# First stage of a decoder trunk: modulation sums by transpose and ScalarE row sums, and two weight buffers moved to multiples of 512 bytes

## The chip, the cores and the metric

The program runs on one NeuronCore of a Trainium2 chip. The metric is the device time of one execution in microseconds (us). Before the change it is 685.16 us, the median of 3 runs (684.44 to 686.75). A core has five engines that each work through their own list of instructions in order and wait for one another by semaphores: TensorE (PE; its weight loads are shown apart as PEld), VectorE (DVE), ScalarE (ACT), GpSimd (POOL) and SyncE (SP, which here only issues transfers). TensorE multiplies a stationary tile, loaded as weights, by a moving tile, and writes into PSUM; all else lies in SBUF, 128 partitions wide.

## The reference

One layer of a decoder on a sequence of 512 tokens with 1024 channels. The part that the change touches is its beginning: a modulation computed from the condition `c`, a normalisation, and the first columns of the input projection.

```python
cs = jax.nn.silu(c)
mod = cs @ w_ada[l] + b_ada[l]
shift1, scale1, gate1, shift2, scale2, gate2 = [m[:, None, :] for m in jnp.split(mod, 6, axis=-1)]
h = _rmsnorm(x, norm1_g[l]) * (1.0 + scale1) + shift1
proj = h @ w_in[l]
...
merged = (jax.nn.sigmoid(ga) * (out_a @ w_branch_swa[l])
          + jax.nn.sigmoid(gd) * (out_d @ w_branch_diff[l]))
x = x + gate1 * (merged @ w_out[l])
```

After the projection come a sliding-window attention and a differential attention, each projected back (`w_branch_swa`, `w_branch_diff`), gated, merged and projected out; then a gated MLP with a short convolution, and a last normalisation. All inputs are float32.

## The kernel before

Channels are cut into eight blocks of 128, numbered k = 0 to 7. The first stage (from about 15 us to 55 us) runs over these blocks and accumulates six PSUM banks `acc6`, each 128 projected columns by 512 tokens. A float32 product is made of three products of fp32r parts: `wh*hTh`, `wl*hTh` and `wh*hTl`, where `wh`/`hTh` are rounded copies and `wl`/`hTl` what the rounding left out. `mm_k(k, 0)` issues the first two products for the banks it is given, `mm_k(k, 2)` the third; so a block costs 18 matmuls of 128x512.

What a block needs before its matmuls:

- The modulation of its 128 channels (`mod`): column 0 a scale, column 1 a shift. Each is a sum over 1024 input channels of `w_ada` times `cs`. The loaded weights `adaw[k]` hold eight slices kk for each of the two sums (j = 0 scale, j = 1 shift). Two partial sums are kept: `ac_1` starts from slice 1 and collects the odd slices, `ac_0` starts from slice 0 and collects the even ones. ScalarE (for k from 3 on) makes the two first products in `ac_first`; VectorE then adds six slices by SCALAR_TENSOR_TENSOR instructions in `ac_ops` (line L301), and adds the two partial sums (L302). What remains is a sum over the 128 partitions: TensorE multiplies `ac_0` as the stationary operand by one column of ones into `pa` (L328). VectorE then adds `1 + bias` to the scale and multiplies by the norm's gain (L334), and ScalarE adds the bias to the shift (L338).
- The turned tokens: `h_turn` transposes four 128x128 tiles of the normalised `x` into PSUM (`xt`, L379).
- `h_tile`: ScalarE applies scale and shift to `xt`, once rounded (`hTA` or `hThB`, called hT below, L384) and once in float32 (`hf`, L384). VectorE subtracts them (`h_low`, L392) and gets `hTl`.
- The weights: ScalarE rounds them (`w0h`, L362 and L364), VectorE subtracts (`w0l`, L370 and L372).

In this stage the lists of TensorE, VectorE and ScalarE stand in the order in which the code is written (`manual_schedule`). In iteration gi of the loop they get the work of block gi and the preparation of block gi+1: TensorE twelve matmuls of block gi, then `pa(gi+1)`, the four transposes of block gi+1, and the six matmuls with `hTl(gi)`; VectorE the six L301, L302, `h_low(gi)`, L334, and the splits of `w0(gi+1)`; ScalarE the two `ac_first` of block gi+2, L338, hT and hf of block gi+1, and the rounding of `w0(gi+2)`. After the stage a scheduler orders the instructions; the first weights of the next projection are rounded by ScalarE (L128, a cast of 128x1024) and subtracted by VectorE (L129). Those two are told to stand behind the instruction `last_mod`, the last one that `finish_mod` returns:

```python
with tc.issue_after(last_mod.ins):
    prefetch()
```

The buffers of the weights of odd blocks (`w0h`, `w0l` for k = 1, 3, 5, 7) lie in the pool `p1`, from byte 198272 of each partition on, which is 128 bytes past a multiple of 512; those of even blocks lie at multiples of 512. Much later (247 us to 303 us) the products with `w_branch_diff` take their weights from `wbd`, at byte 195232, 160 bytes past a multiple of 512. All other stationary operands of 128x512 matmuls lie at multiples of 512. Between the stages named here nothing of the code differs.

Of the kernel before, what the change touches and what calls it, by code (L numbers as in the profile page):

```python
# [8 lines left out]
F32 = mybir.dt.float32  # L9
F32R = mybir.dt.float32r  # L10
AF = mybir.ActivationFunctionType
ALU = mybir.AluOpType
PSUM = bass.MemoryType.PSUM

P = 128
D = 1024
S = 512
KT = D // P
# [42 lines left out]
def kernel(  # L61
# [22 lines left out]
    nc = tc.nc  # L84
# [21 lines left out]
    def tbank(name, shape=(P, S)):  # L106
        return bank("t", 2, list(shape), name)
# [34 lines left out]
    ones = cpool.tile([P, P], F32, name="ones")  # L142
    nc.gpsimd.memset(ones, 1.0)
    ident = cpool.tile([P, P], F32, name="ident")
# [31 lines left out]
    DONE = (0, 4, 2, 5, 1, 3)  # L176
# [42 lines left out]
    pp = pool("p1", stack=p1)  # L219
# [3 lines left out]
    ALONE = 3  # L223
# [50 lines left out]
    cols = cpool.tile([P, NR], F32, name="cols")  # L274
    nc.vector.tensor_copy(cols, pc)
    bsh, bsc1, n1g, sublnc = cols[:, 0:8], cols[:, 8:16], cols[:, 16:24], cols[:, 24:25]
    nc.vector.tensor_scalar_add(bsc1, bsc1, 1.0)
    nc.vector.tensor_scalar_mul(n1g, n1g, -0.5)
    nc.vector.tensor_scalar_mul(sublnc, sublnc, -0.5 * (1.0 - LAM_INIT))
    ac, mods, wts = {}, {}, {}  # L280


    def ac_first(gi, b):
        a = pp.tile([P, 2, P], F32, tag=f"ac{b}", bufs=2, name=f"ac{gi}_{b}")
        aw = adaw[gi]
        if gi < ALONE and b:
            nc.vector.tensor_scalar_mul(a, aw[:, :, b], cs[:, b : b + 1])
        else:
            nc.scalar.activation(a, aw[:, :, b], AF.Copy, scale=cs[:, b : b + 1])
        ac.setdefault(gi, {})[b] = a  # L290

    def ac_ops(gi, low):
        aw = adaw[gi]
        if gi < ALONE:
            ac_first(gi, 1)
        order = (3, 2, 5, 4) if gi == 1 else (3, 5, 2, 7, 4, 6) if gi < ALONE else (3, 2, 5, 4, 7, 6)
        for n, kk in enumerate(order):
            if gi == 1 and n == 1:
                split_lo(0, 1)
            a = ac[gi][kk % 2]  # L300
            nc.vector.scalar_tensor_tensor(a, aw[:, :, kk], cs[:, kk : kk + 1], a, ALU.mult, ALU.add)  # L301
        nc.vector.tensor_add(ac[gi][0], ac[gi][0], ac[gi][1])  # L302
        low()
# [16 lines left out]
    def reduce_mod(gi, early=None):  # L320
        pa = early or tbank(f"pa{gi}", (P, 2, P))
        for j in range(2):
            if early:
                if j:
                    direct(pa, 1, gi, (6, 7))
                nc.tensor.matmul(pa[:, j], ac[gi][0][:, j], ones, start=False, stop=True)
            else:
                nc.tensor.matmul(pa[:, j, 0:1], ac[gi][0][:, j], ones[:, 0:1], start=True, stop=True)  # L328
        return pa

    def finish_mod(k, pa):
        pa = pa if k == 0 else [pa[:, 0], pa[:, 1]]
        m = pp.tile([P, 16], F32, tag="mod", bufs=3, name=f"mod{k}")
        last = nc.vector.scalar_tensor_tensor(  # L334
            m[:, 0:1], pa[0][:, 0:1], bsc1[:, k : k + 1], n1g[:, k : k + 1], ALU.add, ALU.mult
        )
        if k:
            nc.scalar.activation(m[:, 1:2], pa[1][:, 0:1], AF.Identity, bias=bsh[:, k : k + 1])  # L338
        else:
            nc.vector.tensor_add(m[:, 1:2], pa[1][:, 0:1], bsh[:, k : k + 1])  # L340
        mods[k] = m
        return last

    def w0_views(k):
        wh, wl = wts[k]
# [35 lines left out]
    def h_tile(k, between=None):  # L381
        hf = pp.tile([P, S], F32, tag="hf", bufs=2, name=f"hf{k}")
        for dst in (hTh[k], hf):
            nc.scalar.activation(dst, pts[k], AF.Identity, bias=mods[k][:, 1:2], scale=mods[k][:, 0:1])  # L384
            if dst is not hf and between is not None:
                between()
            if dst is not hf and k + 1 < ALONE:
                ac_first(k + 1, 0)
        hfs[k] = hf

    def h_low(k):
        nc.vector.tensor_sub(hTl[k], hfs[k], hTh[k].bitcast(F32))  # L392

    FIRST = (0, 2, 1, 3, 4, 5)

    def mm_k(k, part, some=DONE):
        wh, wl = wts[k]
        last = k == KT - 1
        if part == (2 if last else 1):
            return  # L400
        for i in some:
            for p in (1, 2) if last and part else (0, 1) if part == 0 and not last else (part,):
                lhs, rhs = ((wh, hTh), (wl, hTh), (wh, hTl))[p]
                nc.tensor.matmul(
                    acc6[i], lhs[:, i * P : (i + 1) * P], rhs[k], start=k == 0 and p == 0, stop=last and p == 2
                )
# [28 lines left out]
    def scale_x(t):  # L435
        nc.scalar.activation(xn[:, t, HEAD:], xn[:, t, HEAD:], AF.Copy, scale=rst[:, t : t + 1])
# [46 lines left out]
    for gi in range(KT):  # L483
        more = gi + 1 < KT
        if more:
            if gi == 0:
                scale_x(2)
            split_hi(gi + 1)
            if gi == 1:
                scale_x(3)  # L490
            ac_ops(gi + 1, lambda: h_low(gi))
        else:
            h_low(gi)
            lp = cpool.tile([P, 2, 64], F32, name="lp")
            ls = cpool.tile([P, 2], F32, name="ls")
            nlam = cpool.tile([P, 1], F32, name="nlam")
            nc.vector.tensor_mul(lp, lamv[:, 0:4:2], lamv[:, 1:4:2])
            nc.vector.reduce_sum(ls, lp, axis=mybir.AxisListType.X)
            nc.scalar.activation(ls, ls, AF.Exp)
            nsink = cpool.tile([P, 8], F32, name="nsink")  # L500
            nc.vector.tensor_scalar_mul(nsink, sink, -1.0)
            nc.vector.tensor_sub(nlam, ls[:, 1:2], ls[:, 0:1])
            nc.vector.tensor_scalar_add(nlam, nlam, -LAM_INIT)
        if gi == 0:
            h_turn(1)
        mm_k(gi, 0, DONE if gi else FIRST[:5])
        mm_k(gi, 1)
        if more:
            if gi == 0:
                split_lo(1, 0)  # L510
            pa = reduce_mod(gi + 1, early_mod(1) if gi == 0 else None)
            if gi == 0:
                mm_k(0, 0, FIRST[5:])
            if ALONE <= gi + 2 < KT:
                ac_first(gi + 2, 1)
                ac_first(gi + 2, 0)
            if gi:
                h_turn(gi + 1)
            last_mod = finish_mod(gi + 1, pa)
            if gi:  # L520
                split_lo(gi + 1, 0)
            split_lo(gi + 1, 1)
            h_tile(gi + 1)
        mm_k(gi, 2)
# [503 lines left out]
    for i in range(SWA_PAIRS):  # L1028
        more = i + 1 < SWA_PAIRS
# [66 lines left out]
    bp = pool("mlp")  # L1096
# [32 lines left out]
        units.append((load, branch))  # L1129

    m2 = bp.tile([40, P], F32, name="m2")
    c2 = bp.tile([P, 40], F32, name="c2")
    s2c, a2c = c2[:, 0:8], c2[:, 8:16]
    nc.sync.dma_start(m2[16:32, :], b_ada[0, 3 * D : 5 * D].rearrange("(a p) -> a p", p=P))
    nc.sync.dma_start(m2[32:40, :], norm2_g[0].rearrange("(a p) -> a p", p=P))
# [396 lines left out]
    last = range(KT - TAIL, KT)  # L1532
# [213 lines left out]
    for i, (J, name) in enumerate(slots):  # L1746
# [23 lines left out]
        if i in rows_at:  # L1770
            hf = rows_at[i]
# [329 lines left out]
```

## Time and profile before

| What | Value |
| --- | --- |
| Time, median of 3 runs (lowest to highest) | 685.16 us (684.44 to 686.75) |
| Time of the profiled execution, and its span | 685.38 us, 683.6 us |
| TensorE clock granted over the span | 0.997 |
| Busy share of PE, DVE, ACT, POOL | 99%, 82%, 58%, 14% |
| Transfers | 123.87 MB, mean 181 GB/s |
| Block 3 of the first stage (31.38 to 36.40 us) | 5.02 us |
| Block 4 of the first stage (36.40 to 41.34 us) | 4.94 us |

The span runs from the first to the last instruction; the time of an execution has 1.8 us more around it. A busy PE is not yet a PE at its peak: matmuls overlap, so how closely they follow one another is read from the starts of two neighbours, not from their durations. In a timeline each row gives the start, the duration, the engine, the line, the operation, the tiles written and read, the shape, how many neighbours of the same kind were put into one row, and in brackets the idle time of the engine before it with what ended it.

### The profile page before, as it was taken

How to read it: one execution, taken by the hardware profiler on the slowest of the kernel's cores; microseconds unless marked ns; L12 is line 12 of the kernel's file. 1: busy time of each engine (PE TensorE's matmuls, PEld its weight loads, DVE VectorE, ACT ScalarE, POOL GpSimd, SP SyncE). 2: the span in 40 equal slices, each digit the busy share in tenths (PEclk: the TensorE clock that was granted, in tenths of full speed). 3: DMA queues.
4: the chain of work that ended last, by engine and by line, in shares of the span. 5: the costliest groups of instructions: out<-in, count | busy, mean ns of one | idle time of the engine just before them, and what ended most of it. 6: DMA issues, size and time to landing. Idle time of an engine off the chain costs nothing. (4 is left out here: it accounts for less than half of the span.)

```text
span 683.6 us, 10903 instructions
## 1 busy us (share of the span) xinstructions
PE 673.7 (99%) x4005; PEld 582.2 (85%) x4005; DVE 562.5 (82%) x1075; ACT 398.1 (58%) x722; POOL 98.4 (14%) x119
## 2 busy tenths in 40 slices
PE   8999999999999999999999999999999999999995
PEld 5887887878888888888899999999999998888885
DVE  4999875988796756794589988988888999979997
ACT  6776774546543223233377756666666776656765
POOL 3000000011022011021030101112111102440300
PEclk9999999999999999999999999999999999999998
DMA  9995422565466885469644788886879848995903
GB/s 304 351 301 175 144 62 65 161 167 163 142 159 179 254 245 164 163 187 340 204 89 108 174 195 206 185 184 190 213 163 217 207 146 203 201 204 144 167 1 123
DMA packets 117141, 123.87 MB, mean 181 GB/s; under 512 B 5063, under 2 KB 94184, under 8 KB 117088
## 3 DMA queue, kind: packets, MB, share of 16 engines
q1 hardware_dynamic: 97246, 95.11, 44.2%
q0 software_dynamic: 19648, 27.79, 24.3%
q8 instruction: 31, 0.51, 0.3%
q10 hardware_dynamic: 194, 0.28, 0.1%
q14 instruction: 22, 0.18, 0.1%
HBM read 118.97 MB, written 2.11 MB: 177 GB/s over the span
## 5 line engine op out<-in xcount | busy, mean ns | idle before, releaser
L1390 PE MATMUL up<-t,m_whi 128*128 128x256 f32 x512 | 93.5, 283 | 0.1
L1390 PEld LDWEIGHTS up<-t,m_whi 128*128 128x128 f32 x512 | 79.8, 192 | 0.8 <-ACT up L1427 0.3
L1390 PE MATMUL up<-t,m_wlo 128*128 128x256 f32 x256 | 72.4, 283 | 0.0
L953 POOL DMA_DIRECT2D arow<-arow x28 | 22.5, 802 | 249.1 <-DVE sd L822 123.2
L1390 PEld LDWEIGHTS up<-t,m_wlo 128*128 128x128 f32 x256 | 49.1, 192 | 0.0
L1373 PE MATMUL up<-bhl,p_whi 128*128 128x512 f32 x136 | 48.9, 399 | 0.0
L1272 POOL DMA_DIRECT2D s<-in_w_up_dram x21 | 26.9, 1352 | 144.2 <-DMA s<-in_w_up_dram 65.8
L1302 ACT CAST m_whi<-s 128x1024 fp32r<-128x1024 f32 x31 | 32.6, 1052 | 23.8 <-PE up L1390 10.3
L1306 DVE TENSOR_TENSOR m_wlo<-s,m_whi 128x1024 fp32r<-128x1024 f32 x31 | 37.9, 1221 | 6.0 <-ACT m_whi L1302 5.5
L945 DVE SCALAR_TENSOR_TENSOR arow<-ra,cs,arow 128x512 f32<-128x512 f32 x56 | 41.7, 747 | 0.6
L1377 PE MATMUL up<-bhl,p_wlo 128*128 128x256 f32 x136 | 38.3, 281 | 0.0
L1390 PE MATMUL up<-bhl,p_whi 128*128 128x256 f32 x192 | 35.1, 283 | 0.0
L1390 PE MATMUL up<-t,p_whi 128*128 128x256 f32 x176 | 32.1, 283 | 0.0
L1373 PEld LDWEIGHTS up<-bhl,p_whi 128*128 128x128 f32 x136 | 25.6, 188 | 5.5
L1390 PEld LDWEIGHTS up<-bhl,p_whi 128*128 128x128 f32 x192 | 30.0, 192 | 0.0
L817 ACT ACTIVATE sd<-sd,dmx 128x128 f32<-128x128 f32 (+3 forms) x32 | 17.7, 556 | 17.2 <-DVE dmx L807 17.2
L1390 PEld LDWEIGHTS up<-t,p_whi 128*128 128x128 f32 x176 | 27.4, 191 | 0.4
L1390 PE MATMUL up<-bhl,p_wlo 128*128 128x256 f32 x96 | 27.2, 283 | 0.0
L1377 PEld LDWEIGHTS up<-bhl,p_wlo 128*128 128x128 f32 x136 | 25.7, 189 | 0.0
L1390 PE MATMUL up<-t,p_wlo 128*128 128x256 f32 x88 | 24.9, 283 | 0.0
L1296 DVE TENSOR_TENSOR s<-s,wa 128x1024 f32<-128x1024 f32 x20 | 24.4, 1219 | 0.0
L1397 ACT ACTIVATE gT<-a,cv 128x512 f32<-128x512 f32 x22 | 17.8, 814 | 10.1 <-DVE a L1431 6.2
(501 smaller groups left out, 2085.6 us busy)
## 6 DMA issues: line engine op xcount, KB each, us to landing
ra<-in_w_ada_dram SPq DMA_DIRECT2D x32, 512.0 KB, 4.5
wa<-in_w_up_dram SPq DMA_DIRECT2D x22, 512.0 KB, 4.6
s<-in_w_up_dram SPq DMA_DIRECT2D x21, 512.0 KB, 5.6
s<-in_w_up_dram POOLq DMA_DIRECT2D x21, 512.0 KB, 7.3
w<-in_w_in_dram SPq DMA_DIRECT2D x12, 512.0 KB, 4.8
a<-in_w_up_dram SPq DMA_DIRECT2D x11, 512.0 KB, 4.2
b<-in_w_down_dram SPq DMA_DIRECT2D x10, 512.0 KB, 3.9
adaw<-in_w_ada_dram SPq DMA_DIRECT2D x8, 512.0 KB, 6.8
```

The source lines that it names most:

```text
L817: exp = nc.scalar.activation(pm[m], pm[m], AF.Exp, bias=mx[:, m : m + 1], scale=slope, accum_out=ls)
L945: nc.vector.scalar_tensor_tensor(ac, r[:, a], cc, ac, ALU.mult, ALU.add)
L953: nc.gpsimd.dma_start(whole[0:n], whole[n : 2 * n], accum_op=ALU.add)
L1272: nc.gpsimd.dma_start(dst, upblock(*blk), accum_op=ALU.add)
L1296: nc.vector.tensor_add(src, src, R[J, "a11" if name == "m6" else "a12"])
L1302: nc.scalar.copy(W[J, name][0], R[J, SRC[name]])
L1306: nc.vector.tensor_sub(lo, R[J, SRC[name]], hi.bitcast(F32))
L1373: nc.tensor.matmul(bk, wh[:, k, cu], bhl[:, i, k].rearrange("p b n -> p (b n)"), start=False, stop=k == 3, skip_group_check=True,)
L1377: nc.tensor.matmul(bk[:, :H], wl[:, k, cu], bhl[:, i, k, 0], start=False, stop=k == 3, skip_group_check=True)
L1390: nc.tensor.matmul(o[u], w[:, k, cu], b[:, k], start=opens and k == 0 and x == 0, stop=k == 3 and x == 2, skip_group_check=True,)
L1397: nc.scalar.activation(grow(j), av[J][:, u], AF.Identity, bias=cv[:, 66 + j : 67 + j], scale=cv[:, 44 + j : 45 + j])
```

## The change

For blocks from 2 on the sum over partitions is made in another way. TensorE transposes the two 128x128 halves of `ac_0` into PSUM instead of multiplying them by ones, and two ScalarE passes over 128x128 each sum a row: an activation with `accum_out` writes its result to a scratch tile `spread` and the sum to `mod`. Scale and bias are folded in: the first pass multiplies by the norm's gain, and the biases, divided by 128 because they are added in each of 128 columns, lie ready in a new tile `share`, made once by ScalarE and GpSimd in iteration 1. VectorE's L334 and ScalarE's short L338 go. `spread` has one buffer, so the second pass waits for the first.

Around that: `ac_first(k+1, 0)` moves for blocks from 3 on to a place between hT and hf of block k; the slices are added in the order 3, 5, 2, 7, 4, 6 in all blocks from 2 on; and the matmuls of the sixth bank (`DONE[5:]`, two of them) move from ahead of the transposes of `ac_0` to behind them. `last_mod` becomes a ScalarE instruction. The tile `share` is allocated 384 bytes wide and `c2` 512 bytes wide, which moves what is allocated behind them: `w0h` and `w0l` of odd blocks to 198656 and on, `wbd` to 195584, all multiples of 512.

```diff
+    share = pp.tile([P, 96], F32, name="share")[:, 0:16]
...
-        order = (3, 2, 5, 4) if gi == 1 else (3, 5, 2, 7, 4, 6) if gi < ALONE else (3, 2, 5, 4, 7, 6)
+        order = (3, 2, 5, 4) if gi == 1 else (3, 5, 2, 7, 4, 6)
...
-                nc.tensor.matmul(pa[:, j, 0:1], ac[gi][0][:, j], ones[:, 0:1], start=True, stop=True)
+                nc.tensor.transpose(pa[:, j], ac[gi][0][:, j], ident)
...
-        last = nc.vector.scalar_tensor_tensor(
+        if k > 1:
+            for j, scale, bias in ((0, n1g[:, k : k + 1], share[:, 8 + k : 9 + k]), (1, 1.0, share[:, k : k + 1])):
+                spread = pp.tile([P, P], F32, tag="spread", name=f"spread{k}_{j}")
+                last = nc.scalar.activation(spread, pa[j], AF.Identity, bias=bias, scale=scale, accum_out=m[:, j : j + 1])
+            mods[k] = m
+            return last
+        nc.vector.scalar_tensor_tensor(
...
-            if dst is not hf and k + 1 < ALONE:
+            if dst is not hf and k + 1 < KT:
                 ac_first(k + 1, 0)
...
                 scale_x(3)
+                nc.scalar.activation(share, cols[:, 0:16], AF.Copy, scale=1.0 / P)
+                nc.gpsimd.tensor_tensor(share[:, 8:16], share[:, 8:16], n1g, ALU.mult)
...
-        mm_k(gi, 0, DONE if gi else FIRST[:5])
+        mm_k(gi, 0, DONE[:5] if gi and more else DONE if gi else FIRST[:5])
...
-            if gi == 0:
-                mm_k(0, 0, FIRST[5:])
+            mm_k(gi, 0, (DONE if gi else FIRST)[5:])
             if ALONE <= gi + 2 < KT:
                 ac_first(gi + 2, 1)
-                ac_first(gi + 2, 0)
...
-    c2 = bp.tile([P, 40], F32, name="c2")
+    c2 = bp.tile([P, P], F32, name="c2")[:, 0:40]
```

Line numbers move by one to eight: L289 becomes L290, L301 L302, L302 L303, L328 L329, L379 L385, L384 L390, L404 L410.

How the lists read, first on TensorE in the step from block 5 to block 6 (`a_114` and `a_115` are the banks of the last two columns, `pa` the sums, `xt` the turned tokens), before:

```order
L404 MATMUL a_114<-hTA,w0h_499 128x512
L404 MATMUL a_114<-hTA,w0l_500 128x512
L404 MATMUL a_115<-hTA,w0h_499 128x512
L404 MATMUL a_115<-hTA,w0l_500 128x512
L328 MATMUL pa_573<-ones,ac_0_528 128x1 x2
L379 MATMUL xt_580<-ident,xn 128x128 x4
L404 MATMUL a_110<-hTA,w0h_499 128x512
```

and now:

```order
L410 MATMUL a_114<-hTA,w0h_508 128x512
L410 MATMUL a_114<-hTA,w0l_509 128x512
L329 MATMUL pa_582<-ident,ac_0_551 128x128 x2
L410 MATMUL a_115<-hTA,w0h_508 128x512
L410 MATMUL a_115<-hTA,w0l_509 128x512
L385 MATMUL xt_589<-ident,xn 128x128 x4
L410 MATMUL a_110<-hTA,w0h_508 128x512
```

The two `pa` instructions moved two matmuls up. On VectorE, from the sum of block 6 to that of block 7, before:

```order
L334 SCALAR_TENSOR_TENSOR mod_585<-pa_573,cols 128x1
L370 TENSOR_TENSOR w0l_550<-w_6_170,w0h_549 128x512
L372 TENSOR_TENSOR w0l_550<-w_6_170,w0h_549 128x256
L301 SCALAR_TENSOR_TENSOR ac_1_576<-adaw_172,cs,ac_1_576 128x256
L301 SCALAR_TENSOR_TENSOR ac_0_578<-adaw_172,cs,ac_0_578 128x256
L301 SCALAR_TENSOR_TENSOR ac_1_576<-adaw_172,cs,ac_1_576 128x256
L301 SCALAR_TENSOR_TENSOR ac_0_578<-adaw_172,cs,ac_0_578 128x256
L301 SCALAR_TENSOR_TENSOR ac_1_576<-adaw_172,cs,ac_1_576 128x256
L301 SCALAR_TENSOR_TENSOR ac_0_578<-adaw_172,cs,ac_0_578 128x256
L302 TENSOR_TENSOR ac_0_578<-ac_0_578,ac_1_576 128x256
```

and now:

```order
L376 TENSOR_TENSOR w0l_561<-w_6_170,w0h_560 128x512
L378 TENSOR_TENSOR w0l_561<-w_6_170,w0h_560 128x256
L302 SCALAR_TENSOR_TENSOR ac_1_587<-adaw_172,cs,ac_1_587 128x256 x2
L302 SCALAR_TENSOR_TENSOR ac_0_603<-adaw_172,cs,ac_0_603 128x256
L302 SCALAR_TENSOR_TENSOR ac_1_587<-adaw_172,cs,ac_1_587 128x256
L302 SCALAR_TENSOR_TENSOR ac_0_603<-adaw_172,cs,ac_0_603 128x256 x2
L303 TENSOR_TENSOR ac_0_603<-ac_0_603,ac_1_587 128x256
```

L334 is gone, two slices of `ac_1` come first, and two pairs of neighbours now add into the same tile. On ScalarE, the end of the stage (`mod_631` and `mod_644` are block 7; `w_0_h` are the first weights of the next projection), before:

```order
L364 CAST w0h_599<-w_7_175 128x256
L128 CAST w_0_h<-w_0_703 128x1024
L128 CAST w_0_h<-w_0_709 128x1024
L338 ACTIVATE mod_631<-pa_623,cols 128x1
L384 ACTIVATE hThB<-xt_626,mod_631 128x512
L384 ACTIVATE hf_636<-xt_626,mod_631 128x512
```

and now, with the step of block 6 ahead of it:

```order
L338 ACTIVATE spread_0_595,mod_594<-pa_582,share,cols 128x128
L338 ACTIVATE spread_1_597,mod_594<-pa_582,share 128x128
L390 ACTIVATE hThB<-xt_589,mod_594 128x512
L290 ACTIVATE ac_0_603<-adaw_172,cs 128x256
L390 ACTIVATE hf_601<-xt_589,mod_594 128x512
L368 CAST w0h_612<-w_7_175 128x512
L370 CAST w0h_612<-w_7_175 128x256
L338 ACTIVATE spread_0_645,mod_644<-pa_634,share,cols 128x128
L338 ACTIVATE spread_1_647,mod_644<-pa_634,share 128x128
L128 CAST w_0_h<-w_0_718 128x1024
L390 ACTIVATE hThB<-xt_639,mod_644 128x512
L390 ACTIVATE hf_651<-xt_639,mod_644 128x512
```

The first product of `ac_0` of block 7 stands between hT and hf of block 6, and one of the two long casts moved from ahead of block 7's sums to between them and block 7's hT (the other follows hf). On TensorE the transpose of the convolution's constants, `pcv` (L561, now L567), moved from the end of block 7's matmuls to ahead of them. From the attention on, all lists have the same instructions in the same order as before.

1 line of the change is left out of this document (removed).

## The prediction

> **What bounds the kernel now.** I read the page's busy shares first, then the first stage by windows, then one step of it as a timeline.
>
> ```profile
> PE 673.7 (99%) x4005; PEld 582.2 (85%) x4005; DVE 562.5 (82%) x1075; ACT 398.1 (58%) x722; POOL 98.4 (14%) x119
> ```
>
> ```profile
> 31.38:36.40 5.02, 5.02 (x28) 4.23 (x26) 4.57 (x12) 3.44 (x8) 0.00 (x0) 1.00 1.10 345
> 36.40:41.34 4.94, 4.94 (x28) 4.22 (x26) 4.54 (x12) 3.32 (x8) 0.00 (x0) 1.00 1.10 343
> ```
>
> These two windows are blocks 3 and 4; after the stretch and its length come the busy times of PE, PEld, DVE, ACT. PE is busy throughout at clock 1.00, but VectorE has 4.5 us of work in a 5 us step, so it is close behind. The step from block 5 to block 6:
>
> ```profile
> 43.23 0.42 DVE L302 TENSOR_TENSOR ac<-ac,ac 128x256 f32<-128x256 f32 x1
> 43.90 0.39 PE L404 MATMUL a<-hTA,w0l 128*128 128x512 f32 x1
> 44.13 0.50 PE L328 MATMUL pa<-ones,ac 128*128 128x1 f32 x4
> 44.67 0.22 DVE L334 SCALAR_TENSOR_TENSOR mod<-pa,cols 128x1 f32<-128x1 f32 x1 [0.41 <-PE pa L328]
> 44.92 0.26 ACT L338 ACTIVATE mod<-pa,cols 128x1 f32<-128x1 f32 x1 [1.63 <-DVE mod L334]
> 45.22 0.78 ACT L384 ACTIVATE hThB<-xt,mod 128x512 fp32r<-128x512 f32 x1
> 46.12 0.19 PEld L404 LDWEIGHTS a<-hThB,w0h 128*128 128x128 f32 x1
> 46.35 0.39 PE L404 MATMUL a<-hThB,w0h 128*128 128x512 f32 x1
> ```
>
> The sum `ac` is ready at 43.65, half a microsecond before `pa` starts at 44.13. The chain `pa`, L334, L338, hT ends at 46.00, just ahead of the weight load at 46.12 that needs it. So TensorE waits for nothing: the stage is bound by how closely its matmuls follow one another. Whatever takes TensorE's time here is gained or lost whole, since PE stays 99% busy to the end.
>
> **The change part by part.**
>
> *TensorE's own work.* From the last matmul ahead of `pa` (43.90) to 46.35 lie seven 512-column matmuls at 0.23 (1.61) and the block of `pa` and `xt`: 2.45 - 1.61 = 0.84 us. Transposes alone, from the timeline after the stage (the four between the first two rows, the one between the last two):
>
> ```profile
> 61.04 0.39 PE L134 MATMUL pq<-hTA,w_l 128*128 128x512 f32 x1
> 61.94 0.40 PE L133 MATMUL pq<-hTA,w_h 128*128 128x512 f32 x1
> 55.25 0.39 PE L404 MATMUL a<-hTlB,w0h 128*128 128x512 f32 x1
> 55.82 0.39 PE L133 MATMUL pq<-hTA,w_h 128*128 128x512 f32 x1
> ```
>
> Four cost 0.90 - 2 x 0.227 = 0.45, one 0.57 - 0.45 = 0.12, so two 0.23. Now `pa` and `xt` cost 0.23 + 0.45 = 0.68: 0.16 less, 1.0 us in six steps, if TensorE has nothing else to wait for. A step would then be 4.94 - 0.16 = 4.78.
>
> *What it now waits for.* The two matmuls moved behind `pa` make `pa` due 0.46 us earlier, at a time when `ac` is just ready. And `ac` now hangs on the step before: `pa` of block k, the two ScalarE passes, hT, then `ac_0` of block k+1 (it was made long before), then four VectorE additions and L303, then `pa` of block k+1. One turn of this loop from rows:
>
> ```profile
> 28.58 0.43 DVE L302 TENSOR_TENSOR ac<-ac,ac 128x256 f32<-128x256 f32 x1
> 29.06 0.61 PE L328 MATMUL pa<-ones,ac 128*128 128x1 f32 x4
> ...
> 63.00 0.39 ACT L683 ACTIVATE st<-st,nm 128x128 f32<-128x128 f32 x1
> 63.29 0.18 ACT L683 ACTIVATION_READ_ACCUMULATOR st<-st,nm 128x1 f32 x1
> 63.38 0.50 ACT L683 ACTIVATE st<-st,nm 128x256 f32<-128x256 f32 x1
> ...
> 20.20 0.78 ACT L384 ACTIVATE hTA<-xt,mod 128x512 fp32r<-128x512 f32 x1
> 20.88 0.50 ACT L289 ACTIVATE ac<-adaw,cs 128x256 f32<-128x256 f32 x1
> 21.64 1.27 DVE L301 SCALAR_TENSOR_TENSOR ac<-adaw,cs,ac 128x256 f32<-128x256 f32 x3
> 22.43 1.00 DVE L301 SCALAR_TENSOR_TENSOR ac<-adaw,cs,ac 128x256 f32<-128x256 f32 x2
> 23.46 0.43 DVE L302 TENSOR_TENSOR ac<-ac,ac 128x256 f32<-128x256 f32 x1
> ```
>
> - L303's end (29.01 here) to `pa`: 0.05.
> - `pa` to ScalarE: four passes took 0.61, two with 128 columns lie between 0.39 and 0.53; with 0.04 to wake, 0.48.
> - A summing pass is an ACTIVATE and a READ_ACCUMULATOR: 0.47 from 63.00 to 63.47, and 0.04 until a waiting successor starts. The second pass waits for the first (one `spread`), hT for the second: 1.02. Both read PSUM with scale and bias in tiles, as L338 (0.26 for one column) and hT (0.78 for 512) do: on that line 128 columns are 0.39, the same. I take 1.10; if the wait costs nothing it is 0.81 (twice 63.38 - 63.00, and 0.04), if the passes run as slow as the 256-column one (0.50), 1.24.
> - hT to `ac_0`: 0.68. `ac_0` to VectorE: 0.50 + 0.04.
> - From slice 2 at 21.64 to L302's end: 2.25, in the very order 2, 7, 4, 6 that now holds for all blocks (the first row has 2, 7, 4, the next 4, 6).
>
> Sum: 0.05 + 0.48 + 1.10 + 0.68 + 0.54 + 2.25 = **5.10 us**, against 4.78 of TensorE and the 4.94 to 5.02 of before. The other engines stay below: VectorE has 4.54, less L334, plus twice 0.12 for the neighbours that add into the same tile (0.52 between their starts instead of 0.40), 4.6; ScalarE has 3.4, less L338, plus 1.1, 4.2. No transfer is added or moved. So TensorE would wait some 0.3 us ahead of every `pa`, and the 0.16 of its work is saved for nothing. By the Trainium skill, "ScalarE: Activation LUTs", section "What ACT_TABLE_LOAD costs", an operand in a tile adds about 93 ns each to 186 ns and 0.833 ns a column; an estimate from that page makes the first pass 0.48 instead of 0.39 and the loop 5.2, a further 0.1 per turn.
>
> *Start of the loop.* Block 2's `ac` ended at 23.89, so its `pa` goes at 23.95. Its first pass also waits for `share`: ScalarE makes it after this row, and GpSimd's product follows, for which a one-column one is the nearest:
>
> ```profile
> 22.92 0.94 ACT L436 ACTIVATE xn<-xn,rst 128x768 f32<-128x768 f32 x1
> 11.22 0.55 POOL L195 TENSOR_TENSOR r<-ms,mhalf 128x1 f32<-128x1 f32 x1 [0.61 <-DVE rt L201]
> 47.38 2.01 ACT L128 CAST w_h<-w 128x1024 fp32r<-128x1024 f32 x2
> ```
>
> 23.77 + 0.26 + 0.55 puts the first pass at 24.6 (24.4 without that wait). Then hT 25.7, `ac_0` 26.4, slice 2 26.92, L303's end 29.17, `pa` of block 3 at 29.22: 0.16 behind the 29.06 of before. Four more turns: 29.22 + 4 x 5.10 = 49.62. In the window of block 6, `pa` of block 7 stood 2.21 ahead of 51.29, at 49.08. So **+0.54**.
>
> *Block 7.* One long cast now stands between the second pass and hT, on an engine that works in order; before, both filled ScalarE's idle time at 47.38. Queued behind it are hT and hf, for whom TensorE and VectorE wait. From `pa`: 0.48 to the first pass, 0.51 to the second, 0.38 to the cast, 0.95 for it (2.01 less one of 1.06), 0.78 for hT, 0.05: 3.15 instead of 2.21, **+0.94**. Of that `pcv`, which now runs in this wait, gives 0.12 back, and a restarted first matmul takes up to 0.1. The other cast ends 2.4 us behind hT's start (0.68 until hf, 0.68, 1.05); the first bank that ScalarE has to empty is complete 2.7 behind it (hT's 0.78, eight matmuls of 0.23 and their tail), so it costs nothing.
>
> *The moved buffers.* Odd blocks, whose weights are 128 bytes off, take 5.02 against 4.94: 0.08 each. Later, twelve matmuls with `wbd` (first two rows, from first to next) take 2.80; with `wba`, which is aligned, 2.72:
>
> ```profile
> 247.19 0.39 PE L132 MATMUL pB<-outdA,wbd 128*128 128x512 f32 x1
> 249.99 0.40 PE L132 MATMUL pgd<-hTA,wgd_h 128*128 128x512 f32 x1
> 207.44 0.39 PE L132 MATMUL pA<-outah,wba_h 128*128 128x512 f32 x1
> 210.16 0.39 PE L132 MATMUL pga<-hTA,wga_h 128*128 128x512 f32 x1
> 198.20 0.40 PE L132 MATMUL pA<-outah,wba_h 128*128 128x512 f32 x1
> 199.36 0.39 PE L134 MATMUL pA<-outah,wba_l 128*128 128x512 f32 x1
> ```
>
> With eight such groups **-0.64**. In the first stage the loop hides it in all but block 7: **-0.08**. Against it stand the last two rows: five intervals of 0.232 with aligned weights, so slow pairs have another cause too. Bounds: nothing and 0.96 (0.64 + 4 x 0.08).
>
> *Sum:* 0.54 + 0.94 - 0.12 + 0.1 - 0.64 - 0.08 = **+0.7 us**. The profiled execution would go from 685.38 to 686.1; it stands 0.2 above the median, so the median goes from 685.16 to **685.9**.
>
> **The rivals.**
>
> *TensorE stays the bound.* If the sums wait for nothing (0.81) and the transposes end in 0.39, the loop is 4.72, below 4.78. Then -1.0 for `pa`, -0.96 for the buffers, and +0.7 for block 7 (its chain shorter by 0.1, less `pcv`): -1.2, 683.9. Against it speaks the single `spread`, for it the 0.39-us row.
>
> *The addresses cost nothing*, as the 0.232 in the aligned rows hints: forecast + 0.72, 686.6. This would also follow from the Trainium skill, "SBUF — State Buffer", section "Specifications (TRN2)": its line is 16 bytes, and both old addresses are multiples of that. The 2.80 against 2.72 here disagrees, and decides more for me.
>
> *Slower: the summing passes are dear.* If each takes 0.8 instead of 0.55, as the 512-column read of PSUM does, a turn costs 5.6. Block 3 comes 0.5 later, four turns 2.0, block 7 0.5: with the 0.7 of the forecast +3.7, 688.9. It decides from 0.67 per pass on (+2.1). The ScalarE rows of 0.39 at 128 columns speak against it.
>
> **How the numbers follow.** Forecast 0.46, TensorE-bound 0.24, addresses free 0.18, dear sums 0.12. A measurement of this kernel tells about 0.3% (2.1 us) from no change. The forecast's own range is 684.8 to 687.0. The runs before spread by -0.7 and +1.6 around their median, so each case may land a microsecond off. Faster by over 0.3%, below 683.1: a third of the TensorE-bound case and a little of the others, 0.11. Slower, above 687.2: nearly all of the dear sums, a fifth of the free addresses, a little of the forecast, 0.17. The same: 0.72. The range, from the TensorE-bound case to half way into the dear sums: 683.4 to 687.6.
>
> **What would show it.** Right: `pa` of blocks 3 to 7 follow at about 5.1 us, their weight loads idle some 0.3 us each with L303 as releaser; hT of block 7 starts 1.3 us behind the second pass's start; twelve `wbd` matmuls take 2.72. The forecast is wrong if steps are 4.8 us, if ScalarE's two passes take under 0.9 or over 1.4 together, or if block 7's matmuls start within 2.5 us of its `pa`.

## The result, and the profile after

The changed kernel takes **686.24 us** (median of 22 executions, 684.88 to 692.23); the kernel before, measured beside it, 685.40 (22 executions, 684.44 to 686.83). The ratio is 1.0023, 95% interval 1.0012 to 1.0033: a quarter of a percent on the slow side of no change. Six of the 22 stand above 687.4, where none of before does; the other 16 have a median of 685.91. The profiled execution is the longest of them, 692.23 us with a span of 690.5, so its first stage and what follows are read apart.

**One turn of the loop.** The timeline of the step from block 5 to block 6, after, with the columns of the prediction's timelines:

```profile
45.30 0.44 PE L329 MATMUL pa<-ident,ac 128*128 128x128 f32 x2
45.78 0.46 ACT L338 ACTIVATE spread<-pa,share,cols 128x128 f32<-128x128 f32 x1 [0.93 <-PE pa L329]
46.13 0.19 ACT L338 ACTIVATION_READ_ACCUMULATOR spread<-pa,share,cols 128x1 f32 x1
46.36 0.37 ACT L338 ACTIVATE spread<-pa,share 128x128 f32<-128x128 f32 x1
46.62 0.19 ACT L338 ACTIVATION_READ_ACCUMULATOR spread<-pa,share 128x1 f32 x1
46.85 0.78 ACT L390 ACTIVATE hThB<-xt,mod 128x512 fp32r<-128x512 f32 x1
47.53 0.49 ACT L290 ACTIVATE ac<-adaw,cs 128x256 f32<-128x256 f32 x1
48.06 1.80 DVE L302 SCALAR_TENSOR_TENSOR ac<-adaw,cs,ac 128x256 f32<-128x256 f32 x4 [0.35 <-ACT ac L290]
49.89 0.42 DVE L303 TENSOR_TENSOR ac<-ac,ac 128x256 f32<-128x256 f32 x1
50.37 0.20 PEld L329 LDWEIGHTS pa<-ident,ac 128*128 128x128 f32 x2 [0.46 <-DVE ac L303]
```

From one `pa` to the next are 5.07 us: 0.48 to the first pass, 0.58 to the second, 0.49 to hT, 0.68 to `ac_0`, 0.53 to VectorE's slice 2, 2.25 to the end of L303, 0.06 to `pa`. VectorE waits for `ac_0`, and TensorE's weight load for L303. That wait stands ahead of `pa` of blocks 3 to 7. Three of the four steps between them take 5.07; the one from block 3 to block 4 takes 5.27, because hT starts 0.70 behind the second pass there instead of 0.49. What hT waited for, the profile does not show.

**Block 7.** The same view behind its `pa` at 50.37; the first of the two long casts (L128) stands between the second pass and hT:

```profile
51.42 0.37 ACT L338 ACTIVATE spread<-pa,share 128x128 f32<-128x128 f32 x1
51.78 1.04 ACT L128 CAST w_h<-w 128x1024 fp32r<-128x1024 f32 x1
52.72 0.78 ACT L390 ACTIVATE hThB<-xt,mod 128x512 fp32r<-128x512 f32 x1
52.93 0.24 PE L567 MATMUL pcv<-ident,crow 88*128 88x88 f32 x1
53.55 0.96 PE L410 MATMUL a<-hThB,w0h 128*128 128x512 f32 x3 [0.38 <-ACT hThB L390]
```

**The moved buffers.** Twelve `wbd` matmuls now take 252.54 - 249.82 = 2.72 us, where they took 2.80:

```profile
249.82 0.39 PE L132 MATMUL pB<-outdA,wbd 128*128 128x512 f32 x1
...
252.54 0.39 PE L132 MATMUL pgd<-hTA,wgd_h 128*128 128x512 f32 x1
```

**What makes this execution 692 us long.** Its span is 6.9 us longer than that of before, and 2.1 of them are there by 196 us: from first to last matmul the first stage takes 42.18 us, before 39.53. Half of this difference goes with a wait of ScalarE for a load of weights, 1.29 us at 18.8, which the second profile below does not have. The rest comes after 196 us. First the timeline of before, then of after, at the same four places: the first transfer and the end of a chain of summing transfers that GpSimd issues one after the other (`arow`, sums for later modulation vectors), VectorE's wait for the transfer of `wo`, which SP issues behind another such chain, and the split of the last `wbd`:

```profile
194.75 0.82 POOL L953 DMA_DIRECT2D arow<-arow  x1 [18.33 <-DVE dls L820]
...
224.08 0.52 POOL L956 DMA_DIRECT2D mod_rows<-arow  x1 [1.98 <-DMA arow<-arow]
...
282.59 1.23 DVE L1195 TENSOR_TENSOR wo<-wo,g1b 128x1024 f32<-128x1024 f32 x1 [3.80 <-DMA wo<-in_w_out_dram]
...
296.35 1.22 DVE L129 TENSOR_TENSOR wbd<-wbd,wbd 128x1024 fp32r<-128x1024 f32 x1
```

```profile
196.82 0.82 POOL L959 DMA_DIRECT2D arow<-arow  x1 [18.33 <-DVE dls L826]
...
232.15 0.52 POOL L962 DMA_DIRECT2D mod_rows<-arow  x1 [3.94 <-DMA arow<-arow]
...
287.69 1.23 DVE L1201 TENSOR_TENSOR wo<-wo,g1b 128x1024 f32<-128x1024 f32 x1 [6.68 <-DMA wo<-in_w_out_dram]
...
301.46 1.21 DVE L129 TENSOR_TENSOR wbd<-wbd,wbd 128x1024 fp32r<-128x1024 f32 x1
302.72 0.63 PE L134 MATMUL pB<-outdA,wbd 128*128 128x512 f32 x1 [2.92 <-DVE wbd L129]
```

The first of these chains took 35.3 us instead of 29.3. VectorE came to the split of `wbd` 5.1 us later than before, 3 us of it beyond the 2.1 by which the whole program was late (the first rows), and TensorE stood still for 3.1 us. The clock then took more, as the windows of that stretch show (stretch, length, busy times of PE, PEld, DVE, ACT, POOL, then the granted clock):

```profile
299.20:302.70 3.50, 0.61 (x3) 0.18 (x1) 3.50 (x5) 0.00 (x0) 0.79 (x2) 1.00 0.80 210
302.70:306.14 3.44, 3.42 (x9) 2.64 (x9) 3.44 (x4) 2.06 (x3) 0.61 (x1) 0.54 0.68 201
306.14:308.00 1.86, 1.86 (x9) 1.55 (x8) 1.06 (x3) 0.00 (x0) 0.80 (x1) 0.94 0.00 0
```

For 3.4 us the matmuls followed at 0.43 instead of 0.227: 1.7 us on top of 3.1. By the Trainium skill, "TensorE: Matmul & The Clock Gate", "Part 1: The HAM clock gate", the clock is halved after an idle window of about 3.4 us, until a busy window of that length has passed. The trace agrees on the halved clock, 0.54 for 3.44 us, but not on the idle time: 3.1 us were enough here, and 2.4 us in the trial with two `spread` buffers (0.51 for the next 3.4 us); the measurements decide.

### The profile page after: what moved, and what is told of

It reads as the page before. It is cut to its first block, busy times and chain, and to the rows that moved or that the text cites. A ratio compares the mean times of both kernels' runs of the same rounds, so it can differ in the third digit from the quotient of the medians.

```text
span 690.5 us, 10895 instructions
## 1 busy us (share of the span) xinstructions
PE 676.6 (98%) x3993; PEld 581.4 (84%) x3993; DVE 562.3 (81%) x1069; ACT 402.6 (58%) x741; POOL 99.9 (14%) x120
## 5 line engine op out<-in xcount | busy, mean ns | idle before, releaser
L410 PE MATMUL a<-hTA,w0h 128*128 128x512 f32 x72 | 24.0, 410 | 0.5 <-ACT hTA L390 0.3
```

Source lines behind the costliest of these rows:

```text
L410: nc.tensor.matmul(acc6[i], lhs[:, i * P : (i + 1) * P], rhs[k], start=k == 0 and p == 0, stop=last and p == 2)
```

## The experiments

The theory was that of the prediction: in the first stage a loop of sums, hT, `ac_0` and slices now binds, the cast adds about a microsecond to block 7, and the moved buffers give 0.6 to 1 back. Its rivals: TensorE binds all along, the addresses do nothing, the long executions belong to the change or are chance. "Long" is an execution above 687.4 us, and a step is the time from one `pa` to the next, blocks 3 to 7. Each kernel was measured with the kernel before beside it. The third pass and the two buffers were run once, for their profiles, so their times are no medians.

| Kernel | Median, us (executions) | Ratio to before | Long | Steps, us |
| --- | --- | --- | --- | --- |
| the change again | 689.71 (6) | 1.0066 (1.0043 to 1.0090) | 6 | 5.07, one 5.27 |
| addresses alone | 684.47 (12) | 0.9988 (0.9978 to 0.9997) | 1 | 4.93 |
| `ac_0` early | 685.64 (11) | 1.0026 (1.0005 to 1.0048) | 5 | 4.81 to 5.26 |
| one cast ahead | 686.13 (11) | 1.0027 (1.0003 to 1.0052) | 3 | 5.07, one 5.28 |
| third pass | 693.75 (1) | | 1 | 5.56 |
| order 3, 5, 7, 2, 4, 6 | 686.02 (10) | 1.0029 (1.0003 to 1.0056) | 4 | 4.88, one 5.01 |
| mended, new order | 684.32 (12) | 0.9988 (0.9977 to 0.9999) | 1 | 4.87 |
| mended, `ac_0` early | 684.34 (12) | 1.0001 (0.9982 to 1.0019) | 2 | 4.81 to 5.09 |
| `share` by VectorE | 685.56 (12) | 1.0022 (0.9997 to 1.0048) | 3 | 5.07, one 5.27 |
| `share` by GpSimd, old sums | 684.43 (12) | 0.9988 (0.9978 to 0.9997) | 0 | 4.93 to 5.05 |
| two `spread` buffers | 691.56 (1) | | 1 | 4.95, one 5.28 |
| old sums, delayed | 685.70 (11) | 1.0009 (1.0000 to 1.0018) | 0 | 4.93, then 5.41 |

The kernel before had 1 long execution of 118 beside all these.

**The change again.** No edit.

> The changed kernel once more, for a second profile of it. In its first profile (692.2 us) TensorE stood still for 3.1 us at 302.7, because VectorE had waited 6.7 us for the transfer of wo, which hangs on GpSimd's chain of summing transfers (arow). Theory 'chance': those transfers landed late in that one execution; a profile near the median (686) has no stall over 1 us after 60 us, and the steps of the first stage are 5.1 us again. Rival 'part of the change': the kernel comes to that chain 2 us later and always meets it badly; the stall of about 3 us at wbd is there again, and the profile is above 688.

The stall at `wbd` came again, 3.3 us, and all six executions are long, where 6 of the first 22 were. So it is neither a single accident nor there always. In the first stage of this profile no engine waited for a load, so it serves for the accounts below (first matmul of block 0, `pa` of block 7, its first and its last matmul, then the stall; behind it the first matmul of before, whose `pa` of block 7 is at 49.08 and whose last matmul is at 55.25):

```profile
15.43 0.50 PE L410 MATMUL a<-hTA,w0h 128*128 128x512 f32 x1
...
49.15 0.33 PE L329 MATMUL pa<-ident,ac 128*128 128x128 f32 x1
...
52.33 0.50 PE L410 MATMUL a<-hThB,w0h 128*128 128x512 f32 x1 [0.36 <-ACT hThB L390]
...
56.34 0.39 PE L410 MATMUL a<-hTlB,w0h 128*128 128x512 f32 x1
...
301.79 0.61 PE L134 MATMUL pB<-outdA,wbd 128*128 128x512 f32 x1 [3.11 <-DVE wbd L129]
```

```profile
15.71 0.50 PE L404 MATMUL a<-hTA,w0h 128*128 128x512 f32 x1
```

From first to last matmul the stage takes 40.91 instead of 39.54: **+1.37**.

**Addresses alone.**

```diff
+    share = pp.tile([P, 96], F32, name="share")[:, 0:16]
+    nc.vector.memset(share, 0.0)
...
-    c2 = bp.tile([P, 40], F32, name="c2")
+    c2 = bp.tile([P, P], F32, name="c2")[:, 0:40]
```

> The kernel before with nothing but the two moved allocations (a 384-byte tile share that only holds zeros, and c2 512 bytes wide). Theory of the prediction: twelve wbd matmuls take 2.72 instead of 2.80 in eight groups, -0.64, and the odd blocks of the first stage, which TensorE binds there, 4.94 instead of 5.02, four times -0.08: together -0.96, ratio 0.9986. Rival 'wbd alone': the first stage keeps its mixed matmul intervals of 227 to 236 ns, since such intervals stand in the changed kernel's trace too: -0.64, ratio 0.9991. Rival 'free': ratio 1.0000.

Measured 0.9988, -0.82 us: between the two that believe in the addresses, and off the rival "free". The steps of the first stage, from the timeline's `pa` of block 3 and of block 6:

```profile
28.32 0.50 PE L330 MATMUL pa<-ones,ac 128*128 128x1 f32 x4
...
43.12 0.50 PE L330 MATMUL pa<-ones,ac 128*128 128x1 f32 x4
```

Three steps in 14.80 us, 4.93 each, odd blocks like even ones. So the moved buffers are a gain by themselves, in the first stage too where TensorE binds, and the rest of the change gives it away. The two allocations were not tried one by one.

**`ac_0` early.**

```diff
-            if dst is not hf and k + 1 < KT:
+            if dst is not hf and k + 1 < ALONE:
...
                 ac_first(gi + 2, 1)
+                ac_first(gi + 2, 0)
```

> The changed kernel with ac_0 of the block after next made in its old place, ahead of the summing passes. This takes hT, ac_0 and the four slices out of the loop that I hold to bind the first stage. Loop theory: TensorE no longer waits 0.2 to 0.3 us ahead of pa, so pa of blocks 3 to 7 follow at 4.8 (18 matmuls 4.13, two transposes 0.23, four 0.45) instead of 5.07; five steps give -1.3 us against the changed kernel, so about 685.0. The last block's 3.18 us from pa to its first matmul stay. Rival: the loop is not what binds, the two ac_0 passes ahead of the sums hold ScalarE up instead; steps stay above 5.0 and the time at 686.2.

`pa` of blocks 4 to 7, and what ScalarE does between the first two:

```profile
34.37 0.38 PE L329 MATMUL pa<-ident,ac 128*128 128x128 f32 x2
34.53 0.91 ACT L290 ACTIVATE ac<-adaw,cs 128x256 f32<-128x256 f32 x2 [1.18 <-DVE w0l L376]
39.63 0.38 PE L329 MATMUL pa<-ident,ac 128*128 128x128 f32 x2
44.44 0.38 PE L329 MATMUL pa<-ident,ac 128*128 128x128 f32 x2
49.25 0.38 PE L329 MATMUL pa<-ident,ac 128*128 128x128 f32 x2
```

The last two steps take 4.81: without `ac_0` in the loop nothing waits, and this is TensorE's own step with transposed sums. The first takes 5.26. There ScalarE began its two `ac_first` passes only behind `pa`, after 1.2 us of idle time, and the summing passes stood behind them, so the rival is right in that block. The step before these, from block 2 to block 3, took 5.64, since ScalarE waited for a load of `adaw`. The six executions that are not long have a median of 685.03, as forecast.

**One cast ahead of block 7's passes**, the other behind hf (the casts are told to stand behind VectorE's last split and behind hf):

```diff
-            last_mod = finish_mod(gi + 1, pa)
+            finish_mod(gi + 1, pa)
...
-            split_lo(gi + 1, 1)
-            h_tile(gi + 1)
+            last_mod = split_lo(gi + 1, 1)
+            last_h = h_tile(gi + 1)
...
     with tc.issue_after(last_mod.ins):
+        prefetch(1)
+    with tc.issue_after(last_h.ins):
         prefetch()
```

> The changed kernel with the first of the two 128x1024 casts (L128) put ahead of block 7's summing passes, into ScalarE's 1.3 us of idle time there, and the second behind hf. Theory: from pa of block 7 to its first matmul 3.18 becomes 2.3 (0.48, 1.07, 0.78), steps stay at 5.07: -0.9 us against the changed kernel, about 685.4. Rival: TensorE meets another wait there (VectorE's split of block 7, or the bank that ScalarE empties), and less than 0.4 us is gained.

The timeline of its `pa` of block 2 with the first pass, and of its `pa` of block 7 with the first matmul:

```profile
24.00 0.41 PE L329 MATMUL pa<-ident,ac 128*128 128x128 f32 x2
25.16 0.46 ACT L338 ACTIVATE spread<-pa,share,cols 128x128 f32<-128x128 f32 x1 [0.24 <-POOL share L499]
...
50.24 0.44 PE L329 MATMUL pa<-ident,ac 128*128 128x128 f32 x2
52.82 0.40 PE L411 MATMUL a<-hThB,w0h 128*128 128x512 f32 x1
```

Block 7 takes 2.58, 0.60 less, not 0.9. Without the cast the chain would be through at 2.33, but TensorE has its own work between: the two matmuls that were moved behind `pa`, four transposes and six matmuls of block 6, and it ran without a gap. The median gained nothing, against a forecast of 0.9. In this profile the first pass of block 2 started 1.16 behind its `pa`, since ScalarE made `share` late and GpSimd behind it; in the profile of the change again it started 0.55 behind. So the loop's start costs up to 0.6 us, differently from one execution to the next.

**A third summing pass** in every block from 2 on, into the same place:

```diff
                 last = nc.scalar.activation(spread, pa[j], AF.Identity, bias=bias, scale=scale, accum_out=m[:, j : j + 1])
+            spread = pp.tile([P, P], F32, tag="spread", name=f"spread{k}_2")
+            last = nc.scalar.activation(spread, pa[1], AF.Identity, bias=share[:, k : k + 1], scale=1.0, accum_out=m[:, 1:2])
```

> The changed kernel with a third summing pass behind the second in every block from 2 on (it sums the shift again, into the same place, so nothing else differs). Loop theory: each turn grows by one dependent pass, 0.49 to 0.58, so pa of blocks 4 to 7 follow at 5.55 to 5.65 instead of 5.07, and the first matmul of block 7 stands 3.7 behind its pa instead of 3.18. Rival (TensorE sets the step, the passes lie beside it): there is 0.3 us of room, and steps grow by 0.3 at most.

```profile
34.03 0.44 PE L329 MATMUL pa<-ident,ac 128*128 128x128 f32 x2
...
50.71 0.44 PE L329 MATMUL pa<-ident,ac 128*128 128x128 f32 x2
...
54.38 0.51 PE L412 MATMUL a<-hThB,w0h 128*128 128x512 f32 x1 [0.87 <-ACT hThB L392]
```

Three steps in 16.68 us, 5.56 each, and 3.67 in block 7. Each turn grew by a whole dependent pass, 0.49. ScalarE's passes are on the path; the rival with 0.3 of room is out.

**The slices in the order 3, 5, 7, 2, 4, 6** for blocks from 3 on:

```diff
-        order = (3, 2, 5, 4) if gi == 1 else (3, 5, 2, 7, 4, 6)
+        order = (3, 2, 5, 4) if gi == 1 else (3, 5, 2, 7, 4, 6) if gi < ALONE else (3, 5, 7, 2, 4, 6)
```

> The changed kernel with VectorE's slices of blocks from 3 on in the order 3, 5, 7, 2, 4, 6: the three that need only ac_1 come first, so behind ac_0 stand 2, 4, 6 and L303 (three times 0.52, and 0.43: 1.99) instead of 2, 7, 4, 6 and L303 (2.25). Loop theory: a turn is 0.26 shorter, 4.81, which is TensorE's own 4.81 (measured with ac_0 made early); but VectorE's own work rises by two dependent neighbours of 0.12 to 4.85, so steps of 4.85 to 4.9; five steps save 0.9 to 1.1, about 685.1. Rival: the order is indifferent (VectorE's work, not ac_0, is what pa waits for): steps of 5.07 or more.

`pa` of blocks 4 and 7:

```profile
33.42 0.44 PE L329 MATMUL pa<-ident,ac 128*128 128x128 f32 x2
...
48.06 0.43 PE L329 MATMUL pa<-ident,ac 128*128 128x128 f32 x2
```

Three steps in 14.64, 4.88 each: a step is 0.19 shorter by an order alone, as forecast (4.85 to 4.9). The median is 686.02 only because 4 of 10 executions are long; the six others stand at 684.75.

**Both mended kernels** have one cast ahead, and `share` made by VectorE before block 0; the first adds the new slice order, the second `ac_0` early.

```diff
+    nc.vector.tensor_scalar_mul(share, cols[:, 0:16], 1.0 / P)
+    nc.vector.tensor_mul(share[:, 8:16], share[:, 8:16], n1g)
     finish_mod(0, pa0)
```

> The changed kernel with three things mended: the slices in the order 3, 5, 7, 2, 4, 6; one of the two casts ahead of block 7's passes and one behind hf; share made by VectorE before block 0, so that the first pass of block 2 waits for nothing. Theory: steps 4.85 to 4.9 (-1.0), block 7 2.6 from pa to its first matmul (-0.6), the first pass up to 0.6 earlier where it had waited for share (-0.1 to -0.6): 684.0 or a little above, below the kernel before (685.3) and about the kernel with nothing but the moved allocations (684.5).

> The same mending with ac_0 made in its old place ahead of the passes instead of the new slice order. Theory: undisturbed steps of 4.81; but where a load of adaw lands late, the two ac_first passes hold the sums up, 0.4 us in one or two blocks as in the trial with ac_0 early. So -0.9 to -1.3 for the steps, -0.6 for block 7: 684.0. If the late loads do not recur, 683.7.

The first reaches 684.32, 0.9988 of before (`pa` of blocks 3 and 7 in its timeline, four steps in 19.49):

```profile
28.71 0.42 PE L329 MATMUL pa<-ident,ac 128*128 128x128 f32 x2
...
48.20 0.44 PE L329 MATMUL pa<-ident,ac 128*128 128x128 f32 x2
```

It beats both kernels, but not the addresses alone, which reach the same ratio with two moved allocations. In its execution TensorE still waited 0.8 us for `wbd`. The second had steps of 5.06, 4.81, 5.09, 4.88 and 4.81: the late `ac_first` recurred.

**`share` by VectorE alone, and `share` by GpSimd with the old sums.** The first is the change with the edit just shown (and without ScalarE's and GpSimd's instructions in block 1). The second is the addresses alone with those two instructions instead of the memset:

```diff
+                nc.scalar.activation(share, cols[:, 0:16], AF.Copy, scale=1.0 / P)
+                nc.gpsimd.tensor_tensor(share[:, 8:16], share[:, 8:16], n1g, ALU.mult)
```

> The changed kernel with share made by two short VectorE instructions before block 0 instead of by ScalarE and GpSimd in block 1, nothing else. Two questions. Start of the loop: the first pass of block 2 no longer waits for share (0.2 us of wait and 0.2 of ScalarE in the last profile), at most -0.4. Long executions: those above 687.4 us were 6 of 22, 6 of 6, 5 of 11, 3 of 11 and 4 of 10 in the kernels where GpSimd makes share, 1 of 80, 1 of 12, 1 of 12 and 2 of 12 in those where it does not. Theory 'GpSimd': its added instruction is what shifts the late chain of summing transfers, so at most 1 of 11 is long here and the median is 685.7. Rival 'first stage': the later end of the stage, or the other instructions, shift it; about 4 of 11 stay long.

> The counterpart: the kernel before with the two moved allocations, and share made by ScalarE and GpSimd in block 1 as in the changed kernel, though nothing reads it. Theory 'GpSimd': about 4 of 11 executions are above 687.4 us, as in the changed kernel, and the others stand at 684.5 as with the moved allocations alone. Rival 'first stage': at most 1 of 11 is long.

The theory "GpSimd" falls on both sides: 3 of 12 are long without the added instruction, none of 12 with it. The part that is not long gained 0.7 in the first (685.19 against 685.91), where 0.4 at most was expected.

**Two buffers for `spread`.**

```diff
-                spread = pp.tile([P, P], F32, tag="spread", name=f"spread{k}_{j}")
+                spread = pp.tile([P, P], F32, tag="spread", bufs=2, name=f"spread{k}_{j}")
```

> The changed kernel with two buffers for spread, so that the second pass does not wait for the first. The forecast's sum: the wait costs 0.04 or less, as the pass and its READ_ACCUMULATOR take ScalarE that long anyhow; second pass 0.54 to 0.58 behind the first, steps 5.03 to 5.07. The rival 'TensorE stays bound' had 0.81 for both passes if they wait for nothing: the second 0.40 behind the first, steps 4.9.

The two passes and hT in ScalarE's timeline:

```profile
40.03 0.46 ACT L338 ACTIVATE spread<-pa,share,cols 128x128 f32<-128x128 f32 x1 [0.69 <-PE pa L329]
40.39 0.19 ACT L338 ACTIVATION_READ_ACCUMULATOR spread<-pa,share,cols 128x1 f32 x1
40.48 0.36 ACT L338 ACTIVATE spread<-pa,share 128x128 f32<-128x128 f32 x1
40.73 0.20 ACT L338 ACTIVATION_READ_ACCUMULATOR spread<-pa,share 128x1 f32 x1
40.99 0.78 ACT L390 ACTIVATE hTA<-xt,mod 128x512 fp32r<-128x512 f32 x1
```

Both ends missed: the second pass starts 0.45 behind the first, not 0.54 to 0.58 and not 0.40. The wait for a buffer on the same engine costs 0.13, and three of the four steps are 4.95, 0.12 shorter.

**Old sums, delayed.** The addresses alone, with the transposes of `xt` issued twice in blocks 4 to 7:

```diff
                 h_turn(gi + 1)
+                if gi > 2:
+                    for t in range(NT):
+                        nc.tensor.transpose(pts[gi + 1][:, t * P : (t + 1) * P], xn[:, t, (gi + 1) * P : (gi + 2) * P], ident)
```

> The kernel before with the two moved allocations, and the four transposes of xt issued twice in blocks 4 to 7 (the same values once more): TensorE's stage ends 4 x 0.45 = 1.8 us later, as far as with the changed kernel's first stage, but with the old sums, the old order and no new pass. Theory 'lateness': the late end of the first stage is what brings the executions in which GpSimd's summing transfers land late and TensorE stands still at wbd; 3 to 6 of 12 are then long (688.5 or more), the others at 686.3. Rival 'the new instructions': at most 1 of 12 is long, and the median is 686.3.

The steps grew by 0.48 and the stage ended at 56.91, later than in the profile of the change again (56.34), but none of 11 executions is long. So a late first stage does not bring them by itself. The median is 1.2 us above that of the addresses alone, 0.6 less than forecast; where that went was not followed up.

## Why the prediction was right, point by point

**TensorE binds before.** Right in the first stage: with the addresses alone its step fell from 5.00 (mean of the five in before, from 24.09 to 49.08) to 4.93, and in the end the time followed. But that TensorE's time is "gained or lost whole" goes too far. Near 343 us it waits for VectorE's `xn`, first before, then in the change again:

```profile
343.10 0.74 PEld L1496 LDWEIGHTS th<-ident,xn 128*128 128x128 f32 x7 [0.17 <-DVE xn L1486]
```

```profile
349.13 0.75 PEld L1502 LDWEIGHTS th<-ident,xn 128*128 128x128 f32 x7 [0.58 <-DVE xn L1492]
```

The changed kernel loses 0.4 us there, and so do `ac_0` early and one cast ahead; the addresses alone lose 0.1.

**TensorE's own step, 4.78.** Right in kind, 0.03 off: 4.81 where nothing waits.

**The loop, 5.10.** Right: 5.07, with L303 as releaser, by terms 0.48, 1.07, 0.68, 0.53, 2.25 and 0.06 against 0.48, 1.10, 0.68, 0.54, 2.25 and 0.05. One turn of four is 5.27, so four take 20.48 (20.40 forecast). The third pass moved it by what the sum says, 0.49, the new order by 0.19 of 0.26, to the 4.85 to 4.9 that VectorE's own work was expected to allow. TensorE's loader idles 0.46 ahead of `pa` where I gave 0.3; its step loses 0.26. "TensorE stays the bound" and "dear sums" fall here. By an estimate from the Trainium skill, "ScalarE: Activation LUTs", "What ACT_TABLE_LOAD costs", the first pass is 0.48. The trace has 0.46 and agrees, but the loop did not become 5.2, since what follows a pass is paced by the read of its sum and the wait for the buffer.

**The wait for `spread`.** Mis-sized: 0.04 in the sum, 0.29 in the choice between 1.10 with the wait and 0.81 without it. With two buffers both passes take 0.96 (40.03 to 40.99) instead of 1.07, so the wait costs 0.11 over both, of 0.13 at the start of the second pass. That 1.10 was near 1.07 is in part luck: a wait taken too small and passes taken too dear offset each other.

**Start of the loop, +0.54 until `pa` of block 7.** +0.35 in the profile of the change again (33.72 behind block 0's first matmul, from 15.43 to 49.15, against 33.37). Block 2's `pa` came 0.28 earlier, which I had not counted: its `ac` was ready 0.23 earlier, without the waits for loads that before has there, and `pa` no longer stands behind the two moved matmuls. `share` held the first pass up by 0.1 here and by 0.7 in another execution (the row at 25.16); I had priced it at 0.2.

**Block 7, +0.94.** Right: 3.18 against 3.15 forecast and 2.21 before; hT stands 1.29 behind the second pass's start, where I had said 1.3. What the term did not say is that without the cast only 0.60 of it goes: TensorE's own work from `pa` on, with the two moved matmuls in it, takes 2.58, as the trial with one cast ahead showed. From the first matmul of block 7 to the last are 4.01, before 3.96: 0.09 more in the first six, with the restart, and 0.04 less in the others. So the restart is as forecast, and the aligned weights save half of their 0.08. `pcv` gives 0.12 back behind the last matmul, as forecast.

**The moved buffers, -0.64 and -0.08.** Right in kind, too small for `wbd`. Twelve take 2.72 instead of 2.80 in seven of the eight groups where no stall stands, 2.95 instead of 2.99 in the other: 0.59 with the addresses alone. But from the first of these matmuls to the first of the output projection (L1457 before, L1459 in that run) are 54.82 us (246.04 to 300.86) instead of 55.67 (247.19 to 302.86), 0.85 less. The rest lies in the matmuls right behind each group, which have aligned weights in both kernels: the next eight intervals took 1.85 us before and take 1.81. In the first stage the move gains next to nothing, as forecast. "The addresses cost nothing" falls, and with it, for this case, what I drew from "SBUF — State Buffer" in the Trainium skill: both old addresses are multiples of its 16 bytes, and the move gained 0.82 us.

**The sum, +0.7.** In the profile of the change again the stage is +1.37 and TensorE's work behind it, up to 100 us, -0.25; the stretch with `wbd` is -0.85 where no stall stands in it, and the wait near 343 us +0.4: about +0.7, by terms that the forecast had only in part. The medians differ by 0.84, those of the executions that are not long by 0.51. That the median came out near 685.9 is luck in one respect: no term of the forecast holds the stall, and the six executions of the change again, all with a time above 687.4, have a median of 689.71, beyond the forecast's 687.6.

**The spread.** "Each case may land a microsecond off" was too narrow. 32 of 98 executions of the kernels with the new sums were long, 2 of 153 of those with the old ones, the kernel before among these. The 14 profiles fall into two kinds. In the five above 687.4 us (the change, the change again, third pass, `share` by VectorE, two buffers) the first chain of summing transfers takes 35.3 to 36.5 us, and TensorE stands still for 2.4 to 3.3 us at `wbd`. In the nine others the chain takes 29.1 to 30.6 us, and that stall is 0.8 us once and at most 0.1 in the others. The way from the one to the other is shown: VectorE waits for `wo`, splits `wbd` late, TensorE stands still, and the halved clock adds 1.7 us. Why the chain is slow mostly with the new sums is open. All engines' orders behind the stage are the same. GpSimd's added instruction is not the cause, and a late end of the stage is not enough. Among the kernels with the new sums its end does not decide either: with one cast ahead the stage ended at 56.72 and the chain took 29.1, in the change again at 56.34 and 35.9. The two mended kernels, whose stage is as short as that of before, have 3 of 24.

## What to carry to other kernels

Before an operation is moved behind another one, follow it round: if its result feeds the next turn of that other one, a loop is closed, and its length is a sum of latencies that rows gave here to 0.03 us in three turns of four. A shorter TensorE step is worth nothing beside such a loop, and the order of the adds that hang on its last term is the cheapest way to shorten it. Test the parts of a bundled change alone: here two moved allocations gain 0.1%, and the rest costs more than that. A median over a few executions hides that some of them differ in kind: look at the single times.

## What the runs showed of the hardware

- Where a stationary operand lies matters: 128x512 matmuls follow at 226.7 ns with `wbd` at a multiple of 512 bytes, and at 233.2 on average with it 160 bytes off. Some eight matmuls with aligned weights behind each such group are slowed too, 0.04 us together. Which smaller multiples would do was not tried, nor whether something else that moved with the allocations has a part in it.
- Weights at multiples of 512 bytes are not all: in the first stage neighbouring 128x512 matmuls follow at 230.2 ns on average before, at 227.7 with the addresses alone, and at 230.2 again in the changed kernel, whose weights lie at the same addresses. Why is open.
- A ScalarE pass that sums is two instructions, the pass itself (0.46 or 0.37 us for 128 columns from PSUM) and a read of the sum of 0.19. What waits for either the sum or the scratch buffer starts 0.04 behind the end of that read: 0.58 behind the start of the first pass, 0.49 behind that of the shorter second. With a second buffer the second pass starts 0.45 behind the first.
- A stall of 3.1 us on TensorE cost 4.8, since the clock was granted at 0.54 for the next 3.4 us. In the trial with two `spread` buffers a stall of 2.4 was followed by 0.51, one of 1.6 by 1.00.
- A chain of seven small summing transfers, up to the issue of the one that takes the result, took 29.1 to 30.6 us in nine executions and 35.3 to 36.5 in five, behind the same instructions.
